# Hi and lo weights in two halves of the contraction, and later sums of x, in a decoder trunk on one core

## The chip, the cores and the metric

The kernel runs on one core of a Trainium2 chip. The metric is the device time of one execution in microseconds. The engines are named as in the profile: PE is TensorE (matmuls; PEld are its weight loads), DVE is VectorE, ACT is ScalarE, POOL is GpSimd, SP is SyncE, which here issues the DMAs.

## The reference

Two layers (`DEPTH` 2) on x of 256 tokens by 1024 channels, in float32. Each layer is a feed-forward network (FFN), a mixer, and a second FFN, each followed by a layer norm of `ALPHA * x` plus the branch:

```python
def swiglu(x, w_gate, w_up, w_down):
    return (jax.nn.silu(x @ w_gate) * (x @ w_up)) @ w_down
...
    for l in range(DEPTH):
        x = layer_norm(ALPHA * x + 0.5 * swiglu(x, ffn1_gate[l], ffn1_up[l], ffn1_down[l]), ln_g[l, 0], ln_b[l, 0])
        h = x @ w_in[l]
        ...
        mix = jnp.concatenate([y_pool.astype(x.dtype), y_hgrn.astype(x.dtype)], axis=-1) @ w_out[l]
        x = layer_norm(ALPHA * x + mix, ln_g[l, 1], ln_b[l, 1])
        x = layer_norm(ALPHA * x + 0.5 * swiglu(x, ffn2_gate[l], ffn2_up[l], ffn2_down[l]), ln_g[l, 2], ln_b[l, 2])
```

The hidden width of an FFN is 2816. The mixer pools over windows on one half of its channels and runs a gated linear recurrence on the other. The change does not touch the mixer or the norms.

## The kernel before

**Numbers in two parts.** Every large product is made of float32r operands in a high and a low part (`wh`, `wl` of a weight; `xth`, `xtl` of x). A product takes three matmuls: hi by hi, hi by lo, lo by hi. For each weight tile of 512 KB a DMA fills a raw buffer, ACT casts it to `wh` (line 124), and DVE subtracts `wh` from the raw buffer to make `wl` (line 125). There are five raw buffers in rotation, eight pairs of `wh` and `wl` for gate, up and mixer weights (`NW`), and six for down weights (`ND`). A buffer is handed out in the order in which the program asks.

**The steps of an FFN.** The 2816 hidden columns are 11 groups of 256. A written list, `FIRST` for the first FFN and `ORDER` for the other three, gives the order of steps. `G` makes gate and up of one group and one half of the tokens (x is the stationary operand). `T` is the method `GT`, a *turned* group: the weights are the stationary operand and both halves of the tokens stream past, so the result comes out transposed as the down product wants it. `D` is the down product of a group and a half of the tokens, 12 matmuls. `A` and `B` make two groups (6 and 7) together from sums and differences of blocks of x and of the weights. In all four FFNs the stretch `T2 D1.0 T3 D1.1 T4 D2.0 T5 D2.1 A6.0` occurs; the first FFN begins with `G0.0 T1 D0.0 D0.1`, and groups 8 and 9 are turned too. PE takes its instructions in the program's order; the order on ACT and DVE is laid out by a scheduler that goes by the program's order, priorities and an estimate of what is ready.

**A turned group.** Four weights hold the contraction's eight tiles, two in each. Four PSUM banks named `gu` (all that there are of that name) take gate and up of two blocks of 128 hidden columns. The hi pass goes over the eight tiles with 512 columns (x hi and x lo), four matmuls a tile; then a lo pass with 256 columns over the eight tiles for block 0, and one for block 1. In the groups for which `by_block` holds (group 8, and group 2 except in the first FFN) the hi pass is made for each block by itself too. `gate_turned` empties a block's two banks after its lo pass (copies on ACT, line 553, adds on DVE, line 554), and makes silu, product and the two parts that the down product reads. The next turned group or step A takes the same banks.

**When loads are asked for.** A weight whose last use is in the program calls `used()`; when its count is zero, `advance()` asks for the next weights of one long list, in order, as far as a pair of `wh` and `wl` is free (lines 170 to 173). In a turned group the calls come in the lo pass of block 1, so at the group's end.

**Slots.** `later(n, fn)` runs `fn` when PE's program has advanced by n slots; one slot is 1536 columns, about three matmuls of 512. A turned group is 16 slots, a `D` four.

**The first FFN's sums of x.** Steps A and B read `Sh` and `Sl`, the two parts of four sums and differences of quarters of x. `full_part` makes them: it rebuilds x from its parts in a `cb` buffer (line 218), and once both halves of the tokens are there, it takes a raw buffer, makes four blocks of sums in it on DVE (line 227) and casts and subtracts them to `Sh` and `Sl`. In the first FFN `start` asks for its four calls:

```python
for n in range(4):
    later(SUMMED + 4 * n, lambda n=n: full_part(n % 2, n // 2))
```

The second and the fourth call take a raw buffer each. In the other three FFNs the layer norm before them asks for the sums.

Of the kernel before, what the change touches and what calls it, by code (L numbers as in the profile page):

```python
# [19 lines left out]
S = 256  # L20
DEPTH = 2
KT = D // P
# [24 lines left out]
FINAL = [s[1] for s in ORDER if s[0] == "D" and s[2] == 0][-3:-1]  # L47
SUMMED = 40
TURNS = (5,8,10,11)
PINNED, STARTED = 4, 4  # L50
HT = 8
# [34 lines left out]
def trunk(ctx: ExitStack, tc: tile.TileContext, t, out: bass.AP):  # L86
# [13 lines left out]
    later = Later()  # L100
# [17 lines left out]
    def mm3(ps, lh, ll, wh, wl, start, stop, more=False):  # L118
        for n, (a, b) in enumerate(((lh, wh), (lh, wl), (ll, wh))):
            nc.tensor.matmul(ps, a, b, start=start and n == 0, stop=stop and n == 2, skip_group_check=more)  # L120
        later.tick()

    def halves(dst_h, dst_l, src):
        first = nc.scalar.copy(dst_h, src)  # L124
        return first, nc.vector.tensor_tensor(dst_l, src, dst_h.bitcast(F32), ALU.subtract)  # L125
# [44 lines left out]
    def advance():  # L170
        with tc.high_priority(offset=-BEHIND):
            while position[0] < len(stream) and stream[position[0]].load():
                position[0] += 1
# [37 lines left out]
    def full_part(n, part, pt=None):  # L211

        own = scope[0].tile([P, 4, P], F32, name="cb", bufs=4)
        if pt:
            nc.scalar.copy(own, pt)
        else:
            ks = slice(4 * part, 4 * part + 4)
            nc.vector.tensor_tensor(own, xth[:, n, ks].bitcast(F32), xtl[:, n, ks].bitcast(F32), ALU.add)
        parts_seen[n, part] = own
        if len(parts_seen) == 1:  # L220
            sums[0] = [scope[0].tile([P, 4, KT // 2, P], F32R, name="S" + n) for n in "hl"]
        if (1 - n, part) in parts_seen:
            (a11, a12), (a21, a22) = ([parts_seen[i, part][:, k::2] for k in range(2)] for i in range(2))
            raw = rawp.tile([P, 4, 2, P], F32, name="raw")
            for dst, a, b, op in ((0, a21, a22, ALU.add), (2, a11, a21, ALU.subtract), (1, raw[:, 0], a11, ALU.subtract),
                                  (3, a12, raw[:, 1], ALU.subtract)):
                nc.vector.tensor_tensor(raw[:, dst], a, b, op)
            sh, sl = (s[:, :, 2 * part:2 * part + 2] for s in sums[0])
            halves(sh, sl, raw)
        if len(parts_seen) == 4:  # L230
            parts_seen.clear()
# [121 lines left out]
    class FFN:  # L353
# [155 lines left out]
        def GT(self, g):  # L509

            later.wait(lambda: not self.pending)
            ps = [[psg.tile([P, 2 * S], F32, name="gu") for _ in range(2)] for _ in range(2)]
            n = 0
            for lo in range(2):
                w = S if lo else 2 * S

                blocks = [[0], [1]] if lo or self.by_block(g) else [[0, 1]]
                for block in blocks:  # L520
                    for kt in range(KT):
                        later.wait(lambda: min(xT[0].done, xT[1].done) > kt)
                        weight = self.gw[g][kt // 2]
                        for i in block:
                            for part in range(2):
                                c = (kt % 2) * 512 + part * GW + i * P
                                x = xt2[:, kt].rearrange("p l h t -> p (l h t)")
                                nc.tensor.matmul(ps[i][part][:, 2 * S - w:], weight.parts[lo][:, c:c + P], x[:, 0:w],  # L528
                                                 start=kt == 0 and not lo, stop=kt == KT - 1 and lo == 1)
                                n += w  # L530
                                if n >= 3 * 512:
                                    n -= 3 * 512
                                    later.tick()
                        if kt % 2 and lo and block == [1]:
                            weight.uses = 1
                            weight.used()
                    if lo:
                        self.gate_turned(g, block[0], ps[block[0]])

        def by_block(self, g):  # L540
# [34 lines left out]
        def start(self):  # L575

            ws = self.gw[0]
            for w in ws:
                w.load()
            position[0] = STARTED  # L580
            pinned[0] = 6


            arrived = {}

            def fetch(*pieces):
                for k in pieces:
                    p, name = (rawp, "raw") if k in (3, 5, 6, 7) else (xp, "x")
                    arrived[k] = p.tile([P, 768], F32, name=name)
                    nc.sync.dma_start(arrived[k], t["first"][k])  # L590

            fetch(0, 1, 2, 3)
            for hf in range(2):
                xT[hf] = Transposed(hf, None)
                xT[hf].done = KT
            ps = [[psa.tile([P, 2 * S], F32, name="acc") for _ in range(2)] for _ in range(2)]

            def products(k):
                xs = xt2[:, k].rearrange("p l h t -> p (l h t)")
                for lo in range(2):  # L600
                    w = S if lo else 2 * S
                    for i in range(2):
                        for part in range(2):
                            c = (k % 2) * 512 + part * GW + i * P
                            nc.tensor.matmul(ps[i][part][:, 2 * S - w:], ws[k // 2].parts[lo][:, c:c + P], xs[:, 0:w],
                                             start=k == 0 and not lo, stop=k == KT - 1 and lo == 1)
                for _ in range(2):
                    later.tick()

            def operands(k):  # L610
                w, x = arrived[k][:, 0:512], arrived[k][:, 512:768]
                cs = slice((k % 2) * 512, (k % 2) * 512 + 512)
                wh, wl = (part[:, cs] for part in ws[k // 2].parts)
                xh, xl = (xt2[:, k, n].rearrange("p h t -> p (h t)") for n in range(2))
                lo = lambda l, full, h: nc.vector.tensor_tensor(l, full, h.bitcast(F32), ALU.subtract)
                if k == 0:
                    nc.vector.tensor_copy(xh, x)
                else:
                    nc.scalar.copy(xh, x)
                nc.scalar.copy(wh, w)  # L620
                lo(xl, x, xh)
                lo(wl, w, wh)


            zero = scope[0].tile([P, 256], mybir.dt.bfloat16, name="zero")
            nc.vector.memset(zero, 0.0)
            idle = psg.tile([P, 512], F32, name="gu")[:, 0:256]
            for _ in range(WARM):
                nc.tensor.matmul(idle, zero[:, 0:P], zero, start=True, stop=True)
            with tc.manual_schedule(engines={mybir.EngineType.Activation, mybir.EngineType.DVE}):  # L630
                for k in range(KT):
                    operands(k)
                    fetch(*(4, 5, 6, 7) if k == 0 else ())
                    products(k)
            for w in ws:
                w.uses = 0
            advance()
            for i in range(2):
                self.gate_turned(0, i, ps[i])
            for n in range(4):  # L640
                later(SUMMED + 4 * n, lambda n=n: full_part(n % 2, n // 2))
            self.GT(1)

        def T(self, g, hf, hn):
# [519 lines left out]
```

## Time and profile before

| | |
|---|---|
| median of 3 runs | 943.33 us (941.34 to 944.4) |
| the profiled execution | 944.05 us |
| its span, first to last instruction | 942.3 us |
| granted PE clock | 0.998 |
| PE busy | 930.6 us (99%) |
| DVE busy | 742.5 us (79%) |
| ACT busy | 545.9 us (58%) |
| data read | 190.72 MB, 204 GB/s over the span |

Busy times are of one execution. PE's matmuls overlap and their ends are modelled, so the time of a stretch is best read from one start to the next. A row of a timeline gives the start, the time until the last of its merged instructions ends, engine, line, operation, out and in, shapes, count, and in brackets the engine's idle time before it with what ended it.

### The profile page before, as it was taken

What the parts mean: (1) busy time and instruction counts of PE and PEld (TensorE: products, weight loads), DVE (VectorE), ACT (ScalarE), POOL (GpSimd) and SP (SyncE); (2) the same over time, 40 slices, a digit from 0 to 9 for tenths busy, and PEclk for the clock granted to TensorE, in tenths of its full rate; (3) what the DMA queues carried; (4) which work ended last, traced back from release to release, by engine and by line L of the source; (5) the groups of instructions that cost most, each with busy time, mean ns of one, the idle gap of its engine ahead of it and who ended that gap; (6) DMA issues with size and microseconds to landing.
All of it is one profiled execution on the core that took longest, in us unless ns stands there. A gap on an engine that the chain in (4) does not pass through costs nothing.

```text
span 942.3 us, 13155 instructions
## 1 busy us (share of the span) xinstructions
PE 930.6 (99%) x4767; PEld 789.9 (84%) x4767; DVE 742.5 (79%) x1209; ACT 545.9 (58%) x840; POOL 23.0 (2%) x38
## 2 busy tenths in 40 slices
PE   9999999999999999999999999999999999999996
PEld 7878788888988888888888888888898888888885
DVE  7787978779979768986776589947899797689825
ACT  7765667368446754765446556743975466556720
POOL 0000000010010000000000000000000000000000
PEclk9999999999999999999999999999999999999999
DMA  8855798534525765897327568953417357469801
GB/s 303 317 197 167 261 344 290 194 99 135 207 85 194 270 207 180 288 320 237 128 97 248 175 210 307 329 208 101 139 63 268 111 191 251 167 217 310 317 1 45
DMA packets 55424, 192.62 MB, mean 204 GB/s; under 512 B 6592, under 2 KB 6848, under 8 KB 55360
## 3 DMA queue, kind: packets, MB, share of 16 engines
q1 hardware_dynamic: 55024, 191.14, 59.3%
q8 instruction: 37, 0.61, 0.3%
q0 software_dynamic: 192, 0.53, 0.2%
q14 instruction: 27, 0.22, 0.1%
q10 hardware_dynamic: 144, 0.13, 0.0%
HBM read 190.72 MB, written 1.05 MB: 204 GB/s over the span
## 4 chain that ended last, share of the span: by engine, by line
PE 83%; DVE 7%; DMA 7%; issue 2%; ACT 1%; SPq 0%; DVEq 0%; ACTq 0%
PE gu L120 26%; PE acc L120 26%; PE gu L528 23%; DMA raw<-in_gu 4%; DVE wl L125 2%; PE gu L1002 2%; DMA raw<-in_dn 2%; PE acc L928 1%; PE gu L202 1%; PE acc L874 1%; PE gu L647 1%; DVE hn L556 1%; DMA raw<-in_first 1%; DVE sil L554 0%; ACT wh L124 0%
## 5 line engine op out<-in xcount | busy, mean ns | idle before, releaser
L124 ACT CAST wh<-raw 128x1024 fp32r<-128x1024 f32 x252 | 263.4, 1053 | 169.0 <-DMA raw<-in_gu 61.0
L125 DVE TENSOR_TENSOR wl<-raw,wh 128x1024 fp32r<-128x1024 f32 x252 | 303.7, 1220 | 46.1 <-ACT wh L124 24.1
L120 PE MATMUL gu<-wh,xt 128*128 128x512 f32 x672 | 221.8, 393 | 0.0
L528 PE MATMUL gu<-xt,wh 128*128 128x512 f32 x800 | 187.2, 391 | 1.5 <-DVE sil L554 0.9
L528 PEld LDWEIGHTS gu<-xt,wh 128*128 128x128 f32 x800 | 149.7, 188 | 35.0 <-DVE htl L125 1.5
L120 PEld LDWEIGHTS gu<-wh,xt 128*128 128x128 f32 x672 | 126.0, 188 | 26.4 <-DVE xt L125 0.5
L120 PE MATMUL acc<-dh,hth 128*128 128x512 f32 x354 | 140.2, 396 | 0.0
L120 PE MATMUL acc<-dh,htl 128*128 128x512 f32 x354 | 138.1, 390 | 0.0
L120 PE MATMUL acc<-dl,hth 128*128 128x512 f32 x354 | 137.5, 388 | 0.0
L120 PE MATMUL gu<-wl,xt 128*128 128x512 f32 x336 | 131.1, 390 | 0.0
L125 DVE TENSOR_TENSOR dl<-raw,dh 128x1024 fp32r<-128x1024 f32 x88 | 105.7, 1219 | 23.8 <-ACT dh L124 23.5
L124 ACT CAST dh<-raw 128x1024 fp32r<-128x1024 f32 x88 | 92.0, 1051 | 36.1 <-DMA raw<-in_dn 32.3
L528 PEld LDWEIGHTS gu<-xt,wl 128*128 128x128 f32 x800 | 99.3, 192 | 2.0
L528 PE MATMUL gu<-xt,wl 128*128 128x256 f32 x800 | 99.8, 283 | 0.0
L120 PEld LDWEIGHTS acc<-dh,htl 128*128 128x128 f32 x354 | 66.4, 188 | 14.2
L120 PEld LDWEIGHTS acc<-dl,hth 128*128 128x128 f32 x354 | 66.6, 188 | 12.1
L120 PEld LDWEIGHTS acc<-dh,hth 128*128 128x128 f32 x354 | 66.6, 188 | 11.8
L120 PEld LDWEIGHTS gu<-wl,xt 128*128 128x128 f32 x336 | 63.2, 188 | 12.7
L554 DVE TENSOR_TENSOR sil<-gu,sil 128x256 f32<-128x256 f32 x50 | 20.9, 418 | 37.3 <-ACT sil L553 37.3
L564 ACT ACTIVATE sil<-gu 128x256 f32<-128x256 f32 x20 | 7.7, 383 | 41.7 <-PE gu L120 41.5
L124 ACT CAST hth<-hn 128x256 fp32r<-128x256 f32 x52 | 21.0, 406 | 16.7 <-DVE hn L556 16.0
L314 POOL TENSOR_TENSOR rs<-rs,neghalf 128x1 f32<-128x1 f32 x11 | 10.4, 949 | 741.9 <-DVE rs L313 741.9
(206 smaller groups left out, 1042.9 us busy)
## 6 DMA issues: line engine op xcount, KB each, us to landing
raw<-in_gu SPq DMA_DIRECT2D x196, 512.0 KB, 4.8
raw<-in_dn SPq DMA_DIRECT2D x88, 512.0 KB, 4.7
raw<-in_win SPq DMA_DIRECT2D x40, 512.0 KB, 4.5
raw<-in_wout SPq DMA_DIRECT2D x16, 512.0 KB, 5.0
lng<-in_ln_g SPq DMA_DIRECT2D x6, 512.0 KB, 6.7
lnb<-in_ln_b SPq DMA_DIRECT2D x6, 512.0 KB, 7.6
x<-in_first SPq DMA_DIRECT2D x4, 384.0 KB, 3.7
raw<-in_first SPq DMA_DIRECT2D x4, 384.0 KB, 5.8
```

The costliest lines, as they stand in the source:

```text
L120: nc.tensor.matmul(ps, a, b, start=start and n == 0, stop=stop and n == 2, skip_group_check=more)
L124: first = nc.scalar.copy(dst_h, src)
L125: return first, nc.vector.tensor_tensor(dst_l, src, dst_h.bitcast(F32), ALU.subtract)
L202: nc.tensor.transpose(pt[:, k - a, :], self.nat[:, k * P:(k + 1) * P], ident)
L314: nc.gpsimd.tensor_tensor(rs, rs, neghalf[:, 0:1], ALU.pow)
L528: nc.tensor.matmul(ps[i][part][:, 2 * S - w:], weight.parts[lo][:, c:c + P], x[:, 0:w], start=kt == 0 and not lo, stop=kt == KT - 1 and lo ...
L554: nc.vector.tensor_tensor(dst, p[:, 0:S], dst, ALU.add)
L556: nc.vector.tensor_tensor(h, h, gate, ALU.mult)
L647: nc.tensor.transpose(pt[:, i, :], hn[:, i * P:(i + 1) * P], ident)
L874: nc.tensor.matmul(pe[:, a:], lf[hf][c][:, h * P:(h + 1) * P], cumM[:, c, a:], start=True, stop=True)
L928: nc.tensor.matmul(dst[:, 2 * j:2 * j + 2, :], side[:, j, :], E[:, 2 * j:2 * j + 2, t0:t0 + dst.shape[2]], start=True, stop=True)
L1002: nc.tensor.matmul(ps[i // 2][:, i % 2, :], w, x, start=kt == 0 and n == 0 and i % 2 == 0, stop=kt == KT - 1 and n == 2 and i % 2 == 1)
```

## The change

Turned groups that are not by_block take hi of the first four tiles for both blocks, lo of the same four for both blocks, hi of the last four, and then lo of the last four for block 0 and for block 1. `used()` is called whenever the lo pass has done both blocks of a weight: for the first two weights in the group's middle, for the other two at its end. By_block groups keep their order. In the first FFN the four calls of `full_part` are asked for at slots 66, 72, 78 and 84 after the start, where they were at 40, 44, 48 and 52.

```diff
-SUMMED = 40
+SUMMED = 66
+EARLY = 4
...
-            for lo in range(2):
-                w = S if lo else 2 * S
-
-                blocks = [[0], [1]] if lo or self.by_block(g) else [[0, 1]]
-                for block in blocks:
-                    for kt in range(KT):
+            if self.by_block(g):
+                turns = [(lo, [i], 0, KT) for lo in range(2) for i in range(2)]
+            else:
+                turns = [(lo, [0, 1], 0, EARLY) for lo in range(2)] + [(0, [0, 1], EARLY, KT)]
+                turns += [(1, [i], EARLY, KT) for i in range(2)]
+            for lo, block, first, end in turns:
+                    w = S if lo else 2 * S
+                    for kt in range(first, end):
...
-                        if kt % 2 and lo and block == [1]:
+                        if kt % 2 and lo and 1 in block:
                             weight.uses = 1
                             weight.used()
-                    if lo:
+                    if lo and end == KT:
                         self.gate_turned(g, block[0], ps[block[0]])
...
-                later(SUMMED + 4 * n, lambda n=n: full_part(n % 2, n // 2))
+                later(SUMMED + 6 * n, lambda n=n: full_part(n % 2, n // 2))
```

## The prediction

> **What bounds the kernel now.** I read the page first, then the waits of TensorE, then the turned groups stage by stage, then the queues around the two longest waits.
>
> ```profile
> span 942.3 us, 13155 instructions
> ...
> PE 930.6 (99%) x4767; PEld 789.9 (84%) x4767; DVE 742.5 (79%) x1209; ACT 545.9 (58%) x840; POOL 23.0 (2%) x38
> ...
> L528 PE MATMUL gu<-xt,wh 128*128 128x512 f32 x800 | 187.2, 391 | 1.5 <-DVE sil L554 0.9
> ```
>
> TensorE (PE) is busy for 930.6 of 942.3 us. The other engines can matter only where they make it wait. L528 is the turned group: 800 hi matmuls are 25 groups of 32, each with 32 lo matmuls of 256 columns behind them. By the code, seven of the 25 are by_block groups (group 8 in four FFNs, group 2 in three), and these keep their order. So the change touches 18 groups.
>
> ```profile
> 12.38 1.09 PE L605 MATMUL acc<-xt,wh 128*128 128x512 f32 x4
> 16.60 7.44 PE L528 MATMUL gu<-xt,wh 128*128 128x512 f32 x32
> 23.88 3.99 PE L528 MATMUL gu<-xt,wl 128*128 128x256 f32 x32
> 27.71 0.39 PE L120 MATMUL acc<-dh,hth 128*128 128x512 f32 x1
> ```
>
> Starts, from the timeline of TensorE. An undisturbed group takes 27.71 - 16.60 = 11.11 us: 7.28 for hi, or 0.2275 a matmul, and 3.83 for lo, or 0.1197. The first line is for the price of a switch, below.
>
> ```profile
> 47.02:58.62 11.60, 11.37 (x65) 9.75 (x64) 11.43 (x21) 6.67 (x10) 0.00 (x0) 1.00 0.27 76
> 61.36:73.78 12.42, 11.51 (x66) 9.76 (x64) 7.40 (x14) 8.78 (x16) 0.00 (x0) 1.00 0.69 255
> 76.52:87.62 11.10, 11.10 (x65) 9.83 (x64) 8.30 (x10) 5.13 (x6) 0.00 (x0) 1.00 0.76 238
> 408.22:420.00 11.78, 11.41 (x66) 9.76 (x65) 8.79 (x10) 8.88 (x11) 0.00 (x0) 1.00 0.85 288
> ```
>
> Windows laid on four turned groups (duration; then busy time of PE, PEld, DVE, ACT, POOL; granted clock; DMA share; GB/s). The third takes the undisturbed 11.1. The first is T3 of the first FFN and loses 0.49 us, the second, T4, loses 1.31, and the fourth, a by_block group of the second FFN, 0.67. The rows of T3 tell more: there the DMA share falls to 0.27 and VectorE (DVE) is full, at 11.43 of 11.60.
>
> ```profile
> 101.77 0.39 PE L120 MATMUL gu<-wh,Sl 128*128 128x512 f32 x1
> 102.36 0.50 PE L120 MATMUL gu<-wh,Sh 128*128 128x512 f32 x1 [0.20 <-ACT cb L454]
> ```
>
> Another wait lies between the A and B steps: 0.59 from start to start in place of 0.23, and 0.11 more at the next matmul, so 0.48. These four add up to 2.95 us. That is nearly all that a better order of the supply can win, 0.31% of the span.
>
> **Why T4 waits.**
>
> ```profile
> 61.36 0.63 PE L528 MATMUL gu<-xt,wh 128*128 128x512 f32 x2
> 62.90 1.29 PE L528 MATMUL gu<-xt,wh 128*128 128x512 f32 x4 [0.91 <-DVE sil L554]
> ```
>
> T4's start on TensorE; then ACT and DVE around it:
>
> ```profile
> 58.05 1.05 ACT L124 CAST wh<-raw 128x1024 fp32r<-128x1024 f32 x1 [0.79 <-DMA raw<-in_gu]
> ...
> 60.69 1.05 ACT L124 CAST wh<-raw 128x1024 fp32r<-128x1024 f32 x1 [1.04 <-DMA raw<-in_gu]
> ...
> 61.96 0.35 ACT L553 COPY sil<-gu 128x256 f32<-128x256 f32 x1
> ```
>
> ```profile
> 62.43 0.42 DVE L554 TENSOR_TENSOR sil<-gu,sil 128x256 f32<-128x256 f32 x1
> ```
>
> T4's third matmul needs the bank that T3's block 1 left. The add that empties it starts at 62.43, behind a copy on ScalarE (ACT) at 61.96. T3 had ended at 58.62. The copy stood in ACT's queue behind two casts of T5's weights, and these waited for DMAs.
>
> ```profile
> 42.30 2.38 SPq L151 DMA_DIRECT2D raw<-in_dn  x2
> 54.77 1.43 SPq L151 DMA_DIRECT2D raw<-in_gu  x2
> ```
>
> ```profile
> SPq L151 <- DVE wl L125: 16.4, 5, 10.0
> ```
>
> SyncE's timeline, its wait between 40 and 60 us (in total, times, longest), and DVE:
>
> ```profile
> 49.67 0.76 DVE L227 TENSOR_TENSOR raw<-cb 128x256 f32<-128x256 f32 x2
> ...
> 53.49 1.22 DVE L125 TENSOR_TENSOR wl<-raw,wh 128x1024 fp32r<-128x1024 f32 x1
> 54.63 1.22 DVE L125 TENSOR_TENSOR Sl<-raw,Sh 128x1024 fp32r<-128x1024 f32 x1
> ```
>
> Those DMAs left late. SyncE's queue issued nothing from 44.7 to 54.77, having waited 10.0 us for one wl subtraction. There are five raw buffers in rotation. The code hands them out, at this place, to T4's four weights, D2's two, then the two sums of x, then T5's four. Five places before T5's first stands T4's last weight, and its wl subtraction at 53.49 ends at 54.7: the DMA goes at 54.77. That subtraction is late because the sums (eight short operations at L227 and two Sl subtractions) sit among the wl subtractions from 49.67 on.
>
> **The change, part by part.**
>
> *The passes of a turned group.* No instruction is added or removed. Hi 0-3, lo 0-3, hi 4-7, lo 4-7 has one more pair of switches between 512 and 256 columns in 18 groups. The first group of the kernel alternates at every contraction tile: three tiles take 16.60 - 12.38 = 4.22, so 1.407 each, against 4 x 0.2275 + 4 x 0.1197 = 1.389. A pair costs 0.018, so 18 cost 0.32. The other end is 0, if those 0.018 belong to the start's own waits. A gain is excluded, since the same matmuls run at the same intervals. I take 0.3, the only row with such a switch.
>
> *Weights come free earlier.* Two of a group's four weight tiles are released after 3.64 + 1.92 = 5.56 us and no longer at 11.11. Their wl buffers are last read 4 to 5 us earlier, so half of the four wl subtractions (1.22 each, 2.4 in sum) that now crowd into the end of each group can run in its middle. The wh buffers of tiles 4 to 7 are last read 1.9 us later; they are wanted again two groups on, so this costs nothing. Where groups run undisturbed, TensorE gains nothing from either.
>
> *The sums move from slots 40, 44, 48, 52 to 66, 72, 78, 84.* The counter stands at 16 when they are asked for, so they go from counts 56-68 (T2 to T3) to 82-100 (T4 to T5). They issue no DMA, but their two raw buffers move behind T5's four on SyncE's queue; GpSimd's queue has no part in it. T5's loads are asked for at counts 67, 68 and 76. T5's first raw buffer is now that of T4's second weight. The four adds that rebuild x hold buffers of their own and run as soon as x is there, whatever their slot:
>
> ```profile
> L218 DVE TENSOR_TENSOR cb<-xt x4: 682/682/691, 9.1 to 15.2; 128x512 f32<-128x512 f32 x4
> ```
>
> Times in ns, then the first and last start: these four have ended by 16 us and stay there. The sums' subtractions take eight times about 0.33, start to start, and two times 1.14 on VectorE: 4.9 us. VectorE has 12.42 - 7.40 = 5.0 us idle in T4's window and 11.10 - 8.30 = 2.8 in T5's, 7.8 in all, and the first reader is step A:
>
> ```profile
> 91.75 0.39 PE L120 MATMUL gu<-wh,Sh 128*128 128x512 f32 x1
> ```
>
> So I cost the move at nothing. Without that cover, the late DMA would move to A's weights, at T4's price of 1.3. What queues behind the sums on SyncE now are A's loads.
>
> *T4's wait.* The 10 us hole closes, and T5's first casts no longer block ACT's queue at T3's end: -1.31. *T3's wait* stays: it comes before the moved sums, with loads issued before 44 us whose raw order does not change. *Block 0 of a group ends one lo pass later* (0.96 before the end, in place of 1.92), so the emptying of its banks is squeezed. I cost it at 0, since VectorE has 2.4 us less to do there; the bound is rival three. The waits at 101.8 and 408 stay: bounds -1.15 and, as nothing there is added, 0.
>
> **Sum.** -1.31 + 0.32 = -1.0 us. The profiled execution took 944.05 us (span 942.3 and 1.75 around it), which makes 943.05. The median of the runs, 943.33, is 0.72 below that execution, so the forecast is 942.3.
>
> A page of the Trainium skill says otherwise on the room that is left: Perfetto Trace Analysis, Identifying the Most-Contended Engine, holds that matmul busy time misleads and that LDWEIGHTS busy share shows the distance to the limit. By that rule 16% would be open here, and the sum would not be capped by the waits. The traced groups disagree: 11.1 us each time nothing waits, with weight loads busy for 9.83 of it.
>
> **Rivals.**
>
> *One: the hole only moves.* T5's loads go earlier, but A's loads, now interleaved with the sums' buffers, are late, and TensorE waits 1.3 us at the first A step or T5. For it: five raw buffers stay five. Against: T5's window has a DMA share of 0.76 and 2.8 us of idle VectorE. Time: 943.33 + 0.3 = 943.6.
>
> *Two: all four waits go*, as every queue shifts: 943.33 - 2.95 + 0.3 = 940.7. For it: all four are waits for emptied banks or casts. Against: 408 is a by_block group.
>
> *Three, slower: block 0's later end decides.* Each turned group takes all four gu banks, and the next one wants them 2.74 us later.
>
> ```profile
> 343.99 0.63 PE L528 MATMUL gu<-xt,wh 128*128 128x512 f32 x2
> ```
>
> ```profile
> 343.52 0.42 DVE L554 TENSOR_TENSOR hn<-gu,hn 128x256 f32<-128x256 f32 x1
> ...
> 527.32 0.41 DVE L554 TENSOR_TENSOR hn<-gu,hn 128x256 f32<-128x256 f32 x1
> ...
> 808.28 0.41 DVE L554 TENSOR_TENSOR hn<-gu,hn 128x256 f32<-128x256 f32 x1
> ...
> 90.94 0.41 DVE L554 TENSOR_TENSOR sil<-gu,sil 128x256 f32<-128x256 f32 x1
> ```
>
> These are the next group's start at one place, and the tightest last adds. A next group needs its fourth bank 0.68 after its start, so at 344.67 in the first case, and the add ends at 343.94: 0.73 to spare. By the same reading the next two have 0.54 and 0.56 (their groups start at 527.59 and 808.57), and the last 0.40 before A's third bank is used at 91.75. If ACT and VectorE keep their order, all slip by 0.96: waits of 0.23, 0.42, 0.40 and 0.56, and 0.96 more in T3 and in T4, which wait already. Together 3.5, so 943.33 + 3.5 + 0.3 = 947.2. It decides against the gain once it passes 1.0, that is, from two of the larger places on. Against it: the copies are mostly held by casts, not by TensorE (in T3 the copy at 61.96 comes 3.3 us after the group's end), and two wl subtractions leave that stretch. The skill's Perfetto Trace Analysis, Matmuls, speaks for it: groups should rotate through banks so that emptying one overlaps the next. Here no bank is left to rotate to.
>
> *Four: groups run faster inside*, as the skill's rule on LDWEIGHTS would allow. Mechanism: the intervals shrink until a group takes what its weight loads are busy for, 11.10 to 9.83, in 18 groups: 22.9 us, 920.5. No row shows such a group.
>
> **How the numbers follow.** Forecast 0.47, with its own range of 941.3 to 943.3; rival one 0.24; two 0.12; three 0.14; four 0.02; 0.01 is left. About 0.3% (2.8 us) is what a measurement can tell from no change. Faster, below 940.5: half of rival two, four, and a tail of the forecast with it, 0.12. Slower, above 946.2: most of rival three, 0.11. Between them 0.77. The range of 940.3 to 946.0 holds the forecast, rival one, nearly all of two, and those cases of three in which fewer places wait.
>
> **What would show it.** Right: SyncE issues T5's loads before 52 us, T4 takes about 11.1, changed groups elsewhere 11.13, the Sh casts come after 60 us. Wrong: T4 still above 12 (rival one if A waits instead), or third and fourth matmuls of several groups waiting for L554 (rival three), or groups below 11.0 (four). The forecast fails too if the order on ACT, which is laid out anew for the whole kernel, makes casts wait for DMAs ahead of copies at other places.

## The result and the profile after

| | before | after |
|---|---|---|
| median | 943.03 us (6 runs, 941.34 to 944.4) | 949.31 us (6 runs, 947.7 to 950.14) |
| the profiled execution | 944.05 us | 948.61 us |
| its span | 942.3 us | 946.8 us |

The kernel became slower: after to before is 1.0063, with an interval of 1.0053 to 1.0074. The medians lie 6.3 us apart, the two profiled executions 4.6, since before's is 1.0 above its median and after's 0.7 below. The traces can explain the 4.5 us between the spans.

The page of after. Its L531 is before's L528, the turned group; L557 is the add that was L554, L125 and L126 the cast and the subtraction that were L124 and L125:

```profile
span 946.8 us, 13182 instructions
...
PE 932.5 (98%) x4767; PEld 789.5 (83%) x4767; DVE 744.2 (79%) x1209; ACT 544.5 (58%) x840; POOL 22.7 (2%) x38
...
L531 PE MATMUL gu<-xt,wh 128*128 128x512 f32 x800 | 191.1, 391 | 4.1 <-DVE htl L126 3.1
```

The same matmuls ran, and ACT and DVE worked as long as before to within 2 us. The idle time ahead of the turned groups' hi matmuls went from 1.5 to 4.1 us, and it ends with another releaser: an `htl` subtraction, where it was the add. The waits of PE in after (in total, times, longest) say the same:

```profile
PE gu L531 <- DVE htl L126: 3.1, 2, 1.6
...
PE gu L531 <- DVE sil L557: 0.6, 1, 0.6
...
PE gu L121 <- DVE sil L557: 0.3, 1, 0.3
```

Windows on turned groups of after, with the columns of the prediction's: T3 and T4 of the first FFN, group 8 of the second FFN, T4 of the third FFN, group 8 of the third and of the fourth:

```profile
46.78:58.95 12.17, 11.53 (x66) 9.75 (x64) 11.02 (x18) 9.36 (x14) 0.00 (x0) 1.00 0.79 267
61.69:72.82 11.13, 11.13 (x66) 9.84 (x65) 8.50 (x15) 6.08 (x9) 0.00 (x0) 1.00 0.50 143
407.65:419.03 11.38, 11.38 (x66) 9.77 (x65) 8.27 (x11) 8.14 (x12) 0.00 (x0) 1.00 0.94 328
526.65:537.78 11.13, 11.13 (x65) 9.83 (x64) 7.54 (x12) 5.60 (x9) 0.00 (x0) 1.00 0.55 188
592.06:605.01 12.95, 11.39 (x66) 9.76 (x64) 9.86 (x13) 9.66 (x14) 0.00 (x0) 1.00 0.92 315
875.52:888.45 12.93, 11.36 (x66) 9.76 (x64) 9.77 (x13) 9.66 (x15) 0.00 (x0) 1.00 0.89 320
```

T4 of the first FFN came down from 12.42 to 11.13, as forecast. Most of the loss is in the last two rows: group 8, a by_block group whose passes did not change, takes 12.95 and 12.93. Read the same way, from start to start, the whole difference is this:

| place | before | after | difference |
|---|---|---|---|
| group 8 of FFN 2, 3, 4 | 11.78, 11.25, 11.16 | 11.38, 12.95, 12.93 | +3.07 |
| from T5's end to group 8, FFN 2, 3, 4 | 39.27, 39.27, 39.28 | 39.46, 40.40, 39.81 | +1.85 |
| T4 of FFN 2 | 11.11 | 11.79 | +0.68 |
| T3 of FFN 1 | 11.60 | 12.17 | +0.57 |
| T5 of FFN 2, 4 | 11.11, 11.11 | 11.16, 11.28 | +0.22 |
| T4 of FFN 1 | 12.42 | 11.13 | -1.29 |
| from T5's end to group 8 in FFN 1, with the wait between A and B | 39.81 | 39.27 | -0.54 |
| from the kernel's start to the first turned group | 16.60 | 16.32 | -0.28 |
| switches, 0.02 in each of the 13 changed groups not named above | | | +0.26 |

The sum is +4.5, as between the spans.

**Why group 8 waits.** It takes the four `gu` banks in which four transposes of the step before it stood. They are emptied by four short `hth` casts on ACT and four `htl` subtractions on DVE. In after, PE's timeline at group 8 of the third FFN, then ACT and DVE ahead of it:

```profile
592.06 0.40 PE L531 MATMUL gu<-xt,wh 128*128 128x512 f32 x1
594.02 4.15 PE L531 MATMUL gu<-xt,wh 128*128 128x512 f32 x17 [1.56 <-DVE htl L126]
```

```profile
588.40 1.03 ACT L125 CAST wh<-raw 128x1024 fp32r<-128x1024 f32 x1
589.34 0.42 ACT L498 ACTIVATE cb<-cb 128x256 f32<-128x256 f32 x1
589.66 0.35 ACT L125 CAST hth<-gu 128x256 fp32r<-128x256 f32 x1
589.91 2.00 ACT L125 CAST wh<-raw 128x1024 fp32r<-128x1024 f32 x2
591.81 0.37 ACT L125 CAST hth<-gu 128x256 fp32r<-128x256 f32 x1
```

```profile
591.28 2.35 DVE L126 TENSOR_TENSOR wl<-raw,wh 128x1024 fp32r<-128x1024 f32 x2
593.54 0.42 DVE L126 TENSOR_TENSOR htl<-gu,hth 128x256 fp32r<-128x256 f32 x1
```

The second matmul of the group starts 1.96 after the first, in place of 0.23: a wait of 1.73. Between the first `hth` and the second, ACT casts two weights (589.91); these are group 9's, which nobody needs yet. DVE follows the same order, with two `wl` subtractions of 1.2 each, and reaches the second `htl` at 593.54. ACT and DVE of before, at the same place:

```profile
589.10 0.63 ACT L124 CAST hth<-gu 128x256 fp32r<-128x256 f32 x2
590.09 1.05 ACT L124 CAST wh<-raw 128x1024 fp32r<-128x1024 f32 x1 [0.36 <-DMA raw<-in_gu]
591.04 0.37 ACT L124 CAST hth<-gu 128x256 fp32r<-128x256 f32 x1
```

```profile
590.47 1.21 DVE L125 TENSOR_TENSOR dl<-raw,dh 128x1024 fp32r<-128x1024 f32 x1
...
591.60 0.41 DVE L125 TENSOR_TENSOR htl<-gu,hth 128x256 fp32r<-128x256 f32 x1
```

Before, two `hth` casts run one behind the other and one weight comes after them. ACT and DVE take their instructions in the order that the scheduler laid out; that order differs here, in three FFNs that the diff does not touch at this place. The order alone does not set the loss: the second FFN has the same one in after, but there ACT begins the first `hth` 4.0 us ahead of group 8 (403.65, against 407.65), where it is 2.4 in the third, and group 8 loses 0.27.

**The other new place.** ACT and PE of after, ahead of step A in the third FFN:

```profile
552.69 1.05 ACT L125 CAST wh<-raw 128x1024 fp32r<-128x1024 f32 x1 [2.86 <-DVE raw L246]
553.65 0.37 ACT L556 COPY sil<-gu 128x256 f32<-128x256 f32 x1
```

```profile
554.88 0.50 PE L121 MATMUL gu<-wh,xt 128*128 128x512 f32 x1 [0.33 <-DVE sil L557]
```

A copy that empties T5's bank stands behind a cast that had waited 2.86 for its raw data, and A's matmul waits 0.33 for the add behind that copy. By the starts of the later steps, about 1.0 of the +1.85 is lost at A's start in the three FFNs; the rest is lost at the transposes just ahead of group 8, 0.5 in the third FFN and 0.3 in the fourth.

### The profile page after: what moved, and what is told of

Same layout as the page of the kernel before. It is cut to its first block, busy times and chain, and to the rows that moved or that the text cites. A ratio compares the mean times of both kernels' runs of the same rounds, so it can differ in the third digit from the quotient of the medians.

```text
span 946.8 us, 13182 instructions
## 1 busy us (share of the span) xinstructions
PE 932.5 (98%) x4767; PEld 789.5 (83%) x4767; DVE 744.2 (79%) x1209; ACT 544.5 (58%) x840; POOL 22.7 (2%) x38
## 3 DMA queue, kind: packets, MB, share of 16 engines
HBM read 190.72 MB, written 1.05 MB: 203 GB/s over the span
## 4 chain that ended last, share of the span: by engine, by line
PE 52%; DVE 8%; DMA 6%; issue 2%; ACT 2%; DVEq 0%; ACTq 0%; SPq 0%
PE gu L531 17%; PE acc L121 16%; PE gu L121 15%; DVE wl L126 3%; DMA raw<-in_gu 3%; DMA raw<-in_dn 3%; PE gu L1005 1%; DVE dl L126 1%; ACT dh L125 1%; ACT wh L125 1%; PE acc L931 1%; PE gu L203 1%; PE gu L650 0%; PE acc L877 0%; DVE raw L246 0%
## 5 line engine op out<-in xcount | busy, mean ns | idle before, releaser
L125 ACT CAST wh<-raw 128x1024 fp32r<-128x1024 f32 x252 | 263.1, 1053 | 163.5 <-DMA raw<-in_gu 51.2
L126 DVE TENSOR_TENSOR wl<-raw,wh 128x1024 fp32r<-128x1024 f32 x252 | 303.9, 1222 | 36.6 <-ACT wh L125 26.8
L531 PE MATMUL gu<-xt,wh 128*128 128x512 f32 x800 | 191.1, 391 | 4.1 <-DVE htl L126 3.1
L531 PEld LDWEIGHTS gu<-xt,wh 128*128 128x128 f32 x800 | 148.5, 188 | 37.3 <-DVE htl L126 4.4
L126 DVE TENSOR_TENSOR dl<-raw,dh 128x1024 fp32r<-128x1024 f32 x88 | 105.7, 1221 | 20.1 <-ACT dh L125 19.8
L125 ACT CAST dh<-raw 128x1024 fp32r<-128x1024 f32 x88 | 91.8, 1053 | 35.8 <-DMA raw<-in_dn 31.0
L531 PEld LDWEIGHTS gu<-xt,wl 128*128 128x128 f32 x800 | 101.7, 191 | 3.3
L531 PE MATMUL gu<-xt,wl 128*128 128x256 f32 x800 | 102.6, 283 | 0.0
L557 DVE TENSOR_TENSOR sil<-gu,sil 128x256 f32<-128x256 f32 x50 | 21.0, 420 | 42.6 <-ACT sil L556 42.6
L125 ACT CAST hth<-hn 128x256 fp32r<-128x256 f32 x52 | 20.9, 407 | 18.8 <-DVE hn L559 18.7
```

Source lines behind the costliest of these rows:

```text
L557: nc.vector.tensor_tensor(dst, p[:, 0:S], dst, ALU.add)
```

## The experiments

Theory Q (for the queues) is that the new passes in the later FFNs change the scheduler's estimate, that it therefore lays weight casts ahead of the short operations that empty `gu` banks, and that those casts are the loss. That the estimate is what moved them is inferred from the code and from the orders in the traces; no run shows the scheduler's choice itself. Its rivals: the earlier release of two weights, whose loads come earlier and collide; the moved sums; and the passes themselves, which end block 0 later (rival three of the prediction). Each run was made beside the kernel before on the same chip; the ratios are to it.

**First FFN alone** (first_only): the new passes in the first FFN and the later sums, the old passes elsewhere.

```diff
-            if self.by_block(g):
+            if not self.first and not self.by_block(g):
+                turns = [(0, [0, 1], 0, KT)] + [(1, [i], 0, KT) for i in range(2)]
+            elif self.by_block(g):
```

> The new pass order, the early release and the later sums in the first FFN alone; the other three FFNs keep the old pass order. Theory Q (queue order: the new passes of the later FFNs make the scheduler lay out ACT and DVE anew between step B and the by_block group 8, with weight casts ahead of the halves that free its banks): group 8 of the last two FFNs waits 0.2 us or less as before, the first FFN keeps its gain, time about 941.5 us (943.0 less 1.5), ratio 0.998. Theory R (early loads: whatever is released early crowds the DMA engines and the raw buffers): 6 of 18 groups changed, so about a third of the loss, 945 us. Theory S (block 0's banks are emptied too late): 945 us, with waits at the third and fourth matmuls of T3 and T4.

Measured: 943.12 us, 0.9996 (0.9981 to 1.0010); the gain that was expected with it, to 941.5, is not there. The whole loss goes, so it comes from the later FFNs, from their passes or their earlier release. T4 of the first FFN and group 8 of the third in this run:

```profile
62.15:73.28 11.13, 11.13 (x66) 9.83 (x65) 8.50 (x15) 6.08 (x9) 0.00 (x0) 1.00 0.47 146
590.10:601.43 11.33, 11.33 (x66) 9.76 (x64) 9.71 (x11) 8.14 (x12) 0.00 (x0) 1.00 0.95 325
```

**No earlier release** (no_release): the new passes, with `used()` of all four weights at the group's end.

```diff
-                        if kt % 2 and lo and 1 in block:
-                            weight.uses = 1
-                            weight.used()
+                        if kt % 2 and lo and block == [1]:
+                            for weight in self.gw[g][:2] * (kt == EARLY + 1 and end == KT and first == EARLY) + [weight]:
+                                weight.uses = 1
+                                weight.used()
```

> The changed kernel, but all four weights of a turned group are released at its end, as before; pass order and later sums stay. Its laid-out ACT queue between step B and group 8 is the same as the changed kernel's. Theory Q: group 8 of the last two FFNs still waits 1 to 2 us each, time 948 to 950 us. Theory R: the loss goes, 943 us. Theory S: 949 us, with waits spread over T3 to T5.

Measured: 950.18 us, 1.0064 (1.0040 to 1.0089), as slow as the change. Its group 8s took 12.20, 12.09 and 12.95. The waits of PE in it:

```profile
PE gu L531 <- DVE htl L126: 3.1, 3, 1.6
```

The earlier release has no measurable part.

**Old passes in T4 and T5 of the later FFNs** (old45_later), and **in T5 alone** (old5_later): the branch of first_only with another condition.

```diff
+            if not self.first and g in (4, 5) and not self.by_block(g):
```

```diff
+            if not self.first and g == 5 and not self.by_block(g):
```

> The changed kernel, but groups 4 and 5 of the three later FFNs keep the old passes; groups 3 and 9 of these and the whole first FFN are new. The laid-out ACT queue between step B and group 8 is that of the kernel before. Theory Q: group 8 waits 0.2 us or less in the last two FFNs, time 941 to 943 us. Theory R or S: 12 of 18 groups are still new, so two thirds of the loss stay, 947 us.

> The changed kernel, but group 5 of the three later FFNs keeps the old passes. The laid-out ACT queue before group 8 is a third one: the copy that empties the bank comes ahead of the two down-weight casts again, and the four halves alternate with one weight cast each (half, cast, half, cast, ...). Theory Q, by order alone: the second half stands behind one cast in place of two, so group 8 waits between 0.2 and 0.9 in each of the last two FFNs, and step A no longer waits for group 5's banks: 944 to 946 us. A theory by the number of changed groups (15 of 18 stay new): 948 us.

Measured: 943.71 us, 0.9998 (0.9987 to 1.0009), and 945.89 us, 1.0023 (1.0012 to 1.0035), in that order. With T4 and T5 in the old order, while the other turned groups of these FFNs keep the new passes, group 8 takes 11.55, 11.68 and 11.11, in sum 0.15 more than in before. With T5 alone it takes 11.69, 11.66 and 11.81, and the stretch from T5 to group 8 stays long in the third FFN, at 40.24, though step A had been expected to wait no more. So it isn't the passes as such, and the group that costs time is not the one that was changed: what T4 and T5 do moves a wait that comes 40 us later. On ACT, in the third FFN, old45_later has the order of before between B and group 8; old5_later puts one weight cast after each `hth`, a third order.

**Casts pinned** (pinned_casts, pinned_group9): the change in full; ACT's casts of the last three weights of group 8, or of group 9, and their subtractions on DVE are laid out behind the second of the four `hth` and `htl` ahead of group 8. No wait is added, since the order is kept within one engine.

```diff
-                halves(hth, htl, pt)
+                turned = halves(hth, htl, pt)
+            if not self.first and g in self.pairs | {7} and hf == place.index(0) and g == 7:
+                for w in self.gw[9][1:]:
...
+                        for late, early in zip(w.casts, turned):
+                            tc.add_manual_dep(late.ins, early.ins.name, ...)
```

This is pinned_group9; pinned_casts has `self.gw[8][1:]` in the loop.

> The changed kernel, but the casts and subtractions of the last three weights of group 8 (three later FFNs) are kept behind the halves of the second of the four transposes before it; nothing else differs in the program. Theory Q: group 8's waits of 1.7 us in the last two FFNs fall below 0.5 each, time about 946 us (949.3 less 3 or so). Theories R and S: no gain, 949 us or more.

> The changed kernel, with the casts and subtractions of group 9's last three weights (three later FFNs) kept behind the second half; the order of everything else ahead of group 8 is the changed kernel's, the down casts ahead of the copy included. Theory Q: group 8 waits less than 0.4 us in each FFN, and the waits of step A for group 5's banks (0.2 to 1.1 us) stay: 945 to 946.5 us. Other theories: 949 us.

Measured: 944.54 us, 1.0003 (0.9989 to 1.0017), and 943.74 us, 1.0012 (0.9994 to 1.0030). With all of the change's passes in place, both are back at the time of before, as far as these intervals tell (pinned_group9's leaves room for 2.8 us, and two of its ten runs took 948.21 and 949.07). For pinned_casts about 946 had been expected. Windows on group 8 of the second, third and fourth FFN in pinned_group9:

```profile
409.32:420.43 11.11, 11.11 (x65) 9.83 (x64) 8.35 (x11) 8.29 (x11) 0.00 (x0) 1.00 0.90 320
592.73:603.85 11.12, 11.12 (x65) 9.83 (x64) 8.34 (x9) 7.26 (x10) 0.00 (x0) 1.00 0.88 299
874.21:885.32 11.11, 11.11 (x66) 9.84 (x64) 7.80 (x10) 7.59 (x10) 0.00 (x0) 1.00 0.91 304
```

Its ACT at the same place has the two `hth` casts together again, and the two casts of weights behind them:

```profile
590.34 0.63 ACT L125 CAST hth<-gu 128x256 fp32r<-128x256 f32 x2
590.85 2.01 ACT L125 CAST wh<-raw 128x1024 fp32r<-128x1024 f32 x2
592.75 0.38 ACT L125 CAST hth<-gu 128x256 fp32r<-128x256 f32 x1
```

The casts that stood between are group 9's. ACT of pinned_casts shows why a pin of group 8's casts does the same:

```profile
589.64 0.63 ACT L125 CAST hth<-gu 128x256 fp32r<-128x256 f32 x2
590.16 2.01 ACT L125 CAST wh<-raw 128x1024 fp32r<-128x1024 f32 x2
```

The two `hth` casts are together there too. By the order of the loads, the casts behind them are group 8's own, and group 9's run only after all four `hth`.

**Step A's casts pinned as well** (pinned_both): pinned_group9, with the casts of the first B step's weights behind T5's last copy and add.

```diff
+                if g == 5 and i == 1 and not self.first:
+                    for w in self.gw["B", 6, 0]:
...
+                            for late, early in zip(w.casts, (copied, added)):
```

> As pinned_group9, and the casts of the first step B's two weights are kept behind the copies that empty group 5's banks. Theory Q: both the waits of group 8 and those of step A go, and with new passes, early release and later sums all in place the whole is back at 942.5 to 944.5 us, within 0.2% of the kernel before. If the passes cost by themselves, some 946 us stay.

Measured: 944.33 us, 1.0007 (0.9995 to 1.0018). The stretch from T5 to group 8 took 39.32, 39.28 and 39.57, against 39.52, 39.51 and 39.52 in pinned_group9: 0.4 us less in sum, and no difference in the times. It is within what was expected. pinned_group9 had been expected to keep step A's waits and a time above before's; the stretch's loss shrank from 1.85 to 0.73 in it on its own. How much of the 6.3 us step A holds is therefore not separated.

**Sums alone** (sums_only) and **all but the sums** (early_only): before with the new slots, and the change with the old slots.

```diff
-SUMMED = 40
+SUMMED = 66
...
-                later(SUMMED + 4 * n, lambda n=n: full_part(n % 2, n // 2))
+                later(SUMMED + 6 * n, lambda n=n: full_part(n % 2, n // 2))
```

> The kernel before with the later sums (slots 66, 72, 78, 84) and nothing else: old passes and late release everywhere. The prediction's step that closing the 10 us hole in the DMA queue saves T4's wait: T5's loads leave before 52 us, T4 takes 11.1, time 941.7 us (943.0 less 1.3). If T4's wait of the one profiled execution is not in the usual execution, or moves to T5 or step A: 943 us, within 0.5 of the kernel before.

> The new passes and the early release everywhere, with the sums of x at the old slots 40 to 52. The laid-out ACT queue before group 8 of the three later FFNs is that of the changed kernel. Theory Q (queue order): group 8 waits 1 to 2 us in the last two FFNs and the whole is 948 to 951 us, as the changed kernel or a little above it. If the later sums had part in the loss: 944 to 946 us.

Measured: 943.65 us, 0.9997 (0.9987 to 1.0007), and 949.74 us, 1.0068 (1.0052 to 1.0084). The sums have no part in the loss, and bring no gain that the times show, where 941.7 had been expected of them alone. SyncE's timeline of sums_only shows what they move; T5's loads leave at 48.20, not 54.77:

```profile
48.20 12.46 SPq L151 DMA_DIRECT2D raw<-in_gu  x6
```

**Hi whole, lo in halves** (hi_whole): hi over all eight tiles, then lo of the first four for both blocks, then the rest of lo block by block. Two weights are still released earlier, and there is one switch as before.

```diff
-                turns = [(lo, [0, 1], 0, EARLY) for lo in range(2)] + [(0, [0, 1], EARLY, KT)]
-                turns += [(1, [i], EARLY, KT) for i in range(2)]
+                turns = [(0, [0, 1], 0, KT), (1, [0, 1], 0, EARLY)] + [(1, [i], EARLY, KT) for i in range(2)]
```

> The changed kernel with another order of passes: hi of all eight tiles, then lo of the first four for both blocks, then lo of the last four by block; early release of the first two weights remains. The laid-out ACT queue before group 8 has two weight casts between the first and the second half, as in the changed kernel, and one down cast ahead of the copy in place of two. Theory Q: group 8 waits 1 to 2 us in the last two FFNs, 947 to 949.5 us. If the split of the hi pass itself costs: 943 to 944 us.

Measured: 946.75 us, 1.0038 (1.0023 to 1.0052). Its waits of PE:

```profile
PE gu L530 <- DVE htl L126: 2.6, 3, 0.9
```

Undisturbed groups take 11.11 here, but group 8 takes 12.32, 12.17 and 12.24. ACT in the third FFN:

```profile
589.22 0.35 ACT L125 CAST hth<-gu 128x256 fp32r<-128x256 f32 x1
...
590.15 1.98 ACT L125 CAST wh<-raw 128x1024 fp32r<-128x1024 f32 x2
592.04 0.36 ACT L125 CAST hth<-gu 128x256 fp32r<-128x256 f32 x1
```

Two weight casts stand between the first `hth` and the second, as in after, but none just ahead of the first, where after has one (588.40). The waits are shorter and come in all three FFNs, and the time is just below the 947 to 949.5 that was expected.

**The cause without the change** (before_pushed): the kernel before, with nothing of the change; the second half of those `hth` and `htl` is laid out behind the casts and subtractions of two of group 9's weights.

```diff
+            if not self.first and g == 7 and hf == place.index(0):
+                for w in self.gw[9][1:3]:
+                    for late, early in zip(turned, w.casts):
+                        tc.add_manual_dep(late.ins, early.ins.name, ...)
```

> The kernel before, old passes and old sums, with one thing taken from the changed kernel's queues: in the three later FFNs the second of the four halves ahead of group 8 is kept behind the casts and subtractions of group 9's second and third weights, so that three of group 9's casts stand before it, as in the changed kernel. Theory Q (queue order): the loss comes without any change of passes; group 8 waits 2 to 4 us in each of the three FFNs and the whole is 948 to 953 us. Every theory that blames the passes, the early release or the sums themselves: no loss, 943 to 944 us.

Measured: 960.82 us, 1.0183 (1.0160 to 1.0206), the right sign and place, but 17 us where 4 to 9 were expected. Windows on its group 8 of the second, third and fourth FFN, and PE's timeline at the second of them, up to 609 and then up to 612 us:

```profile
408.88:426.14 17.26, 13.00 (x66) 10.89 (x64) 11.71 (x13) 12.07 (x16) 0.00 (x0) 0.90 0.89 307
598.39:616.32 17.93, 14.21 (x65) 11.86 (x64) 11.94 (x14) 11.48 (x15) 0.00 (x0) 0.81 0.84 293
886.06:903.48 17.42, 13.84 (x65) 11.52 (x64) 11.75 (x14) 11.75 (x15) 0.00 (x0) 0.80 0.87 305
```

```profile
602.51 6.73 PE L529 MATMUL gu<-xt,wh 128*128 128x512 f32 x16 [3.72 <-DVE htl L125]
...
602.51 9.69 PE L529 MATMUL gu<-xt,wh 128*128 128x512 f32 x29 [3.72 <-DVE htl L125]
```

Two things made it dearer than in after. Three casts and three subtractions come to stand between the first half and the second, where after has two (on DVE 3.49 us in the third FFN, against 2.35), and the first of these casts waits 0.3 to 3.1 us for its DMA; so PE waits 3.7 to 4.4 us a time, not 1.7. And the granted clock falls to 0.80 to 0.90 in these windows (more on this at the end). This run shows that the order alone makes the wait; its size isn't that of after.

No version was measurably faster than the kernel before.

## Why the prediction was wrong

The forecast was 942.3, with a range up to 946.0, and "slower" at 0.11. It came out at 949.31, above every rival's time too; the slowest was 947.2.

**T4's wait of 1.31 goes: right in the trace, not in the times.** T4 takes 11.13, and SyncE's timeline of after has T5's loads leave at 45.00, not 54.77, as forecast ("before 52 us"):

```profile
41.70 2.35 SPq L152 DMA_DIRECT2D raw<-in_dn  x2
45.00 15.36 SPq L152 DMA_DIRECT2D raw<-in_gu  x8
```

first_only has that gain without the loss, and comes to 0.9996 (0.9981 to 1.0010); sums_only, 0.9997. A gain of 1.3 us is 0.14%, which these intervals can barely tell from nothing. T4 itself still took 11.77 in sums_only's trace, where 11.1 had been expected. The profiled executions of first_only and before differ by 1.51 us (942.54 and 944.05), the medians by 0.24 (943.12 and 943.36): the execution of before that the sum was made against was one of its slower ones. Whether its wait is shorter in the others can't be read, since each kernel has one trace.

**The switch at 0.018: right.** Undisturbed groups with three switches take 11.13, with one 11.11: 0.02.

**The moved sums at nothing: right as a cost.** sums_only stays at before's time, early_only at after's.

**Rival three: right in two places of the six that it priced.** T4 of the second FFN lost 0.68, for which 0.23 was the price. PE and DVE of after:

```profile
342.51 0.63 PE L531 MATMUL gu<-xt,wh 128*128 128x512 f32 x2
343.50 3.48 PE L531 MATMUL gu<-xt,wh 128*128 128x512 f32 x14 [0.36 <-ACT hth L125]
```

```profile
341.46 1.22 DVE L126 TENSOR_TENSOR wl<-raw,wh 128x1024 fp32r<-128x1024 f32 x1
...
343.27 0.41 DVE L557 TENSOR_TENSOR hn<-gu,hn 128x256 f32<-128x256 f32 x1
```

The third matmul starts at 343.50, where 342.97 was due, and the last add, at 343.27, comes only after the group's start; before, it came 0.47 ahead. The slip is more than the 0.96 of the price, and DVE's order has part in it: the `wl` subtraction at 341.46 stands ahead of block 1's adds, where before one came behind them (343.86). T3 of the first FFN, priced at 0.96 more, lost 0.57: its third matmul waits 0.6 for such an add, behind a cast on ACT that had waited 0.76 for its DMA. T4 of the first, third and fourth FFN and step A of the first show no such wait. So the squeeze is real at the tightest places and came to 1.25 us of the 3.5 priced. It isn't the loss: pinned_group9 keeps block 0's later end in every changed group, and in its trace T4 of the second FFN (12.10) and T3 of the first (13.01) take even longer than in after, yet its time is 1.0012 (0.9994 to 1.0030).

**The step that failed** is the one that cost the passes in the later FFNs at 0 beside the switches and left group 8 as it was: "The waits at 101.8 and 408 stay: bounds -1.15 and, as nothing there is added, 0". The wait at 408 is that of group 8 in the second FFN. The step took for granted that ACT and DVE keep their order around the groups. The front part says that this order is laid out by a scheduler that goes by an estimate; the prediction let it shift on the fast side, in rival two, and on the slow side only in its last sentence on failure, with neither a price nor a chance. It had a price in the rows: four banks that group 8 takes are emptied by operations of 0.4 us, which stand in one queue with casts and subtractions of 1.05 and 1.22. Two of these ahead of an `htl` make 2.4 us, and group 8 of the second FFN had already lost 0.67 in this way. In three FFNs that is up to 7 us, all of it on the slow side.

The term missing from the sum measured +3.07 at group 8 and +1.85 between T5's end and group 8 in the profiled execution. By the times of first_only, old45_later and the pinned runs the cause as a whole is worth what was lost, about 6 us. The traces carry 4.5 of the loss; whether the rest is the same waits, longer in other executions, stays open.

## What to carry to other kernels

Where a scheduler lays out queues from an estimate, an edit to one engine's loop can change the order on the others at places that the diff doesn't touch: find the banks with no spare and the short operations that empty them, and price one or two long operations ahead of each as a rival on the slow side. When a change loses time, compare the order of each queue ahead of the new waits first; pinning the few instructions that matter tells an order's cost apart from the change's own. A wait of about 1 us in one profiled execution is not yet a gain of 1 us in the median.

## What the runs showed of the hardware that was not expected

In before_pushed a wait costs more than its own length. After PE's 3.72 us of idle time in the third FFN the next 16 matmuls take 6.73 us, that is (6.73 - 0.40) / 15 = 0.42 from start to start, and the 13 after these 2.96, or 0.23 each. That is 15 x 0.195, or 2.9 us more. These windows are laid on the stretches at the lower clock in the second, third and fourth FFN (duration; busy time of PE; granted clock; DMA share; GB/s). On both sides of each the granted clock is 1.00:

```profile
413.99:417.41 3.42, 3.42 (x10) 0.50 0.90 307
601.73:608.56 6.83, 6.05 (x14) 0.50 0.95 341
888.45:895.28 6.83, 5.25 (x12) 0.50 0.93 349
```

Their starts lie 187.74 and 286.72 us apart, which is 55 times 3.4135 and 84 times 3.4133, and their lengths are one time and two times 3.42. So in this trace the clock changes on one grid of 3.41 us that does not begin with the wait: in the second FFN it fell 0.46 us after PE had begun again (413.53). What a wait costs beside its own length depends on where it lies on the grid: 1.7, 2.9 and 2.6 us here, after 4.26, 3.72 and 3.58 us of idle time. The idle time of 1.56 in after left the clock at 1.00; the traces shown here have no wait between these.

The Trainium skill (TensorE: Matmul & The Clock Gate, What's actually happening) says that the PE's clock is halved after at least one idle window of about 3.4 us, that it comes back after at least one busy window of that length, and that these windows run free of the kernel. The trace agrees on the halved rate, the length and the free run; the window that ended at 413.99 halved the clock though PE was busy for its last 0.46 us.
